# A recurrent branch's projection as seven block products, run two tiles at a time under attention

## The chip, the cores and the metric

One core of one Trainium2 chip runs the whole kernel. The metric is the device time of one execution in microseconds; for the kernel before it is 2162.91 us, the median of three runs (2162.57 to 2163.46).

The engines, by the names that the profile uses: PE is TensorE (matrix products; PEld is its loading of weights), DVE is VectorE, ACT is ScalarE, POOL is GpSimd, SP is SyncE, which only issues transfers. ACTq, POOLq and SPq are the queues from which ScalarE, GpSimd and SyncE issue transfers. Each engine has its own list of instructions, with semaphores between the lists. Sums of matrix products are formed in PSUM, in tiles of 128 x 512 numbers that this text calls banks.

## The reference

A decoder block over 2048 positions and 1024 channels, in float32. One input projection gives eight parts: the input and gate of a recurrent branch, queries, keys, values and a gate of an attention branch, and two merge gates.

```python
x_rnn, z_rnn, q, k, v, z_attn, g_r, g_a = jnp.split(h @ w_in, IN_SPLITS, axis=-1)
hr = rg_lru(causal_depthwise_conv(x_rnn, conv_w, conv_b), ...)
y_rnn = (hr * silu(z_rnn)) @ w_out_rnn            # 2048 x 1024 @ 1024 x 1024
o = dilated_attention_mixture(rope(q), rope(k), v)
y_attn = (o * silu(z_attn)) @ w_out_attn
merged = sigmoid(g_r + bg_r) * y_rnn + sigmoid(g_a + bg_a) * y_attn
x = x + gate * (merged @ w_o)
return rms_norm(x, g_final)
```

The change concerns `y_rnn`, the product with `w_out_rnn`.

## The kernel before

**Precision.** A number is split into a high and a low part, both of type float32r (`hi_act`, `hi_dve` or a VectorE reduction for the high part; `lo_pool` on GpSimd or `lo_dve` on VectorE for the rest), and a product of two such pairs is three matmuls, `mm3`: high x high, high x low, low x high. One `mm3` over 128 x 128 weights and 512 columns is called a step here.

**Positions** are held in four banks of 512 columns, n = 0 to 3. The input projection is done in two halves f = 0, 1 of two banks each. `values_half` forms the values (and, in `build_odd`, the operands of the odd bank and the sums `T1` to `T4`); then 28 pairs of weight columns follow in `strassen`, seven block products each where plain blocks would need eight. Their weight operands are split on the way (tiles `S`, a ring of `NS` = 7). In the second half the operands of the first 20 pairs come back from a copy in DRAM, `sD`, loaded by `load_next` as ring tiles come free. `recurrent` finishes the recurrent branch and stores it, transposed, in DRAM as `yaT` (1024 x 2048).

The order of the work is written out: `late` and `after_prod` list functions to be called after the nth block product (`n_prod`), `later(d, fn)` puts one d products ahead. `values_half` is the exception: there a scheduler orders the instructions.

In the second half more is put beside the products. `output_weights` loads both output projections' weights, splits them and stores the pairs to DRAM in `wD` (one half tile every four products: load at 1, split at 4, store at 5, with the split held in the one-buffered tiles `s1`, `s2`). `residual_gate` forms the residual gate's row from `w_mod`.

**Attention** comes next, in slots: a list of 96 units (16 heads and halves, six units each) runs through stages several slots apart. In each slot TensorE does the scores of one unit, the transposes of a unit seven slots older and the weighted sums of one eight slots older; VectorE and ScalarE do the softmax and copy out of PSUM. Between them the generator `fill` is advanced: it is the output projection, one step at each `next`. `FILL` says how many steps a slot is owed; `spend` takes them at three places of a slot, two after the scores and one after the transposes.

`fill` is made by `steps(jobs)`. A job is a bank n of one branch; a tile is 128 rows m of its output, eight steps over k, summed in one of two PSUM banks of the pool `pjb` (tiles `pj`). The weights come by `load_w` (one transfer of 512 KB for four steps, three tiles ahead, four buffers), the operand by `load_y` and `split_y` (256 KB per k, once for each bank). `evict` multiplies a finished sum by its gate (`load_g`) with VectorE, at step 1 of the next tile, and `store` writes it to `mrT`. The jobs are the four banks of `yaT`, then four of `oT` (the attention branch). The first five banks, 320 steps, go under attention and a few steps of them behind it; the last three run afterwards with other work, and then comes the final projection with w_o.

```python
fill = steps([(0, yaT, n) for n in range(NB)] + [(1, oT, n) for n in range(NB)])
...
mm3(ps[:], wt[:, 0, k % KH, :], wt[:, 1, k % KH, :], yh[:], yl[:], first=k == 0, last=k == KT - 1)
```

## Time and profile before

| | us |
|---|---|
| median of three runs | 2162.91 |
| the profiled execution | 2161.23 |
| its span, first to last instruction | 2159.4 |
| PE busy | 2136.6 (99%) |
| PEld busy | 1788.3 (83%) |
| DVE busy | 1463.3 (68%) |
| ACT busy | 1296.2 (60%) |
| POOL busy | 1120.6 (52%) |

The mean granted TensorE clock is 0.998. The stages lie so: the first half's values and products to about 690 us, the second half's values to 785, its products to 1340, attention with the projection beside it from 1340 to 1866, the rest of the projection to 1999, the final projection to the end.

How to read rows: a group is "line engine operation, output<-inputs by the program's names, partitions x elements, xcount | busy us, mean ns of one | idle time of the engine just before them, and what ended it". A row of busy times by stage is "from:to length, busy us (xinstructions) of PE, PEld, DVE, ACT and POOL, granted clock, share of the DMA engines' time, GB/s". A row of waits is "who <- whom: us in total, times, longest". A timeline row is "start, us, engine, line, operation, tiles, xcount [idle before]". L152 is `mm`, L163 `hi_dve`, L166 `lo_pool`, L169 `lo_dve`, L160 `hi_act`, L1795 `evict`, L1777 the high part in `split_y`, L1480 the softmax's first pass.

### The profile page before, as it was taken

The numbers are of one execution on the slowest core, as the hardware profiler recorded it, in microseconds if no ns is written. First come the engines' busy times: TensorE is split into PE (matmuls) and PEld (weight loads), VectorE is DVE, ScalarE is ACT, GpSimd is POOL, SyncE is SP. The second block draws the span as 40 slices with busy tenths as digits, with TensorE's granted clock in tenths as the row PEclk, the third lists the DMA queues.
The fourth block names the chain that finished last, engine by engine and source line by source line (L and its number), as shares of the span: only waits on it lengthen the run. The fifth ranks groups of instructions, "written<-read, shape, count | busy, mean of one in ns | idle before, by whom it ended". The sixth has DMA issues, their size and how long they took to land.

```text
span 2159.4 us, 32571 instructions
## 1 busy us (share of the span) xinstructions
PE 2136.6 (99%) x10539; PEld 1788.3 (83%) x10539; DVE 1463.3 (68%) x2582; ACT 1296.2 (60%) x2592; POOL 1120.6 (52%) x868
## 2 busy tenths in 40 slices
PE   9999999999999999999999999999999999999998
PEld 6888778888888888888888887889898988878887
DVE  6759878768656715544436684587777687788777
ACT  5748668668644527457457532677788888443333
POOL 1467667777666423223223675466666664432555
PEclk9999999999999999999999999999999999999999
DMA  8467887887655368899997676888887777899543
GB/s 301 142 211 256 280 290 264 288 294 244 174 115 166 108 229 291 301 305 311 323 318 240 152 173 171 300 269 263 273 275 218 256 236 239 300 316 300 181 170 114
DMA packets 416575, 521.39 MB, mean 241 GB/s; under 512 B 107574, under 2 KB 282898, under 8 KB 415380
## 3 DMA queue, kind: packets, MB, share of 16 engines
q1 hardware_dynamic: 376388, 401.65, 59.7%
q10 hardware_dynamic: 34384, 99.78, 12.2%
q0 software_dynamic: 5632, 17.88, 2.6%
q8 instruction: 83, 1.36, 0.3%
q14 instruction: 88, 0.72, 0.1%
HBM read 332.02 MB, written 187.17 MB: 240 GB/s over the span
## 4 chain that ended last, share of the span: by engine, by line
PE 71%; DVE 4%; DMA 3%; issue 1%; POOL 1%; ACT 1%; SPq 0%; ACTq 0%; POOLq 0%; DVEq 0%
PE X L152 14%; PE V L152 13%; PE pj L152 12%; PE Z L152 7%; PE W L152 7%; PE Y L152 6%; PE sc L152 4%; PE o L152 4%; PE pg L152 1%; PE pT L1568 1%; PE pT L1581 1%; DMA fg<-gaT 1%; DMA kraw<-kqT 1%; DVE ptl L169 1%; DVE yl L169 1%
## 5 line engine op out<-in xcount | busy, mean ns | idle before, releaser
L166 POOL TENSOR_TENSOR S<-R,S 128x512 fp32r<-128x512 f32 x192 | 295.3, 1546 | 169.3 <-ACT S L160 82.9
L152 PE MATMUL V<-T,S 128*128 128x512 f32 x1344 | 324.3, 390 | 1.9 <-DVE ev L461 1.9
L152 PE MATMUL X<-T,S 128*128 128x512 f32 x1344 | 323.8, 390 | 1.6 <-ACT u L391 1.3
L152 PE MATMUL pj<-yh,S 128*128 128x512 f32 x896 | 321.6, 402 | 1.3 <-DVE fg L1795 0.8
L152 PEld LDWEIGHTS X<-T,S 128*128 128x128 f32 x1344 | 251.8, 188 | 56.5 <-ACT u L391 2.9
L152 PEld LDWEIGHTS V<-T,S 128*128 128x128 f32 x1344 | 251.9, 188 | 55.9 <-issue 1.9
L166 POOL TENSOR_TENSOR S<-s,S 128x512 fp32r<-128x512 f32 x116 | 173.3, 1494 | 150.1 <-ACT S L160 114.3
L152 PEld LDWEIGHTS pj<-yh,S 128*128 128x128 f32 x896 | 168.3, 188 | 32.3 <-DVE S L169 1.3
L1481 ACT ACTIVATE pp<-pp,st 128x256 f32<-128x256 f32 (+3 forms) x256 | 133.8, 524 | 78.0 <-DVE st L1480 77.4
L152 PE MATMUL pj<-yl,S 128*128 128x512 f32 x448 | 175.5, 392 | 1.0 <-POOL yl L166 1.0
L160 ACT ACTIVATE S<-s 128x512 fp32r<-128x512 f32 x124 | 77.3, 624 | 145.1 <-DVE s L291 92.1
L152 PE MATMUL W<-T,S 128*128 128x512 f32 x672 | 161.6, 389 | 0.0
L152 PE MATMUL Y<-T,S 128*128 128x512 f32 x672 | 161.6, 389 | 0.0
L152 PE MATMUL Z<-T,S 128*128 128x512 f32 x672 | 161.4, 389 | 0.0
L160 ACT ACTIVATE S<-R 128x512 fp32r<-128x512 f32 x200 | 121.5, 622 | 59.0 <-DMA R<-in_w_in_dram 14.8
L169 DVE TENSOR_TENSOR ptl<-pT,pth 128x384 fp32r<-128x384 f32 (+1 forms) x160 | 97.8, 628 | 80.5 <-ACT pth L160 78.4
L152 PEld LDWEIGHTS W<-T,S 128*128 128x128 f32 x672 | 126.0, 188 | 26.9 <-issue 0.9
L152 PEld LDWEIGHTS Z<-T,S 128*128 128x128 f32 x672 | 126.2, 188 | 26.2
L152 PEld LDWEIGHTS Y<-T,S 128*128 128x128 f32 x672 | 126.1, 188 | 26.1
L166 POOL TENSOR_TENSOR s<-R,s 128x512 fp32r<-128x512 f32 x32 | 43.2, 1350 | 188.8 <-ACT s L160 164.6
L980 DVE SCALAR_TENSOR_TENSOR xc<-xr,par,xc 128x512 f32<-128x512 f32 x96 | 102.0, 1062 | 52.1 <-ACT xc L974 49.9
L1548 ACT ACTIVATE pp<-pp,M 128x256 f32<-128x256 f32 (+3 forms) x256 | 118.0, 523 | 12.8 <-DVE M L1680 12.8
(419 smaller groups left out, 4906.0 us busy)
## 6 DMA issues: line engine op xcount, KB each, us to landing
sD<-S ACTq DMA_DIRECT2D x140, 512.0 KB, 3.7
S<-sD SPq DMA_DIRECT2D x140, 512.0 KB, 5.0
S<-wD SPq DMA_DIRECT2D x82, 512.0 KB, 5.5
R<-in_w_in_dram SPq DMA_DIRECT2D x144, 256.0 KB, 3.3
wD<-s ACTq DMA_DIRECT2D x64, 256.0 KB, 5.1
kraw<-kqT SPq DMA_DIRECT2D x32, 384.0 KB, 5.1
T<-in_w_mod_dram SPq DMA_DIRECT2D x16, 512.0 KB, 9.1
vN<-ev SPq DMA_DIRECT2D x32, 256.0 KB, 2.7
```

Source lines behind the costliest of these rows:

```text
L152: nc.tensor.matmul(o, lhsT=l, rhs=r, start=st, stop=sp, **kw)
L160: nc.scalar.activation(o, i, AF.Copy)
L166: nc.gpsimd.tensor_tensor(o, i, h.bitcast(F32), ALU.subtract)
L169: return nc.vector.tensor_tensor(o, i, h.bitcast(F32), ALU.subtract).ins
L980: nc.vector.scalar_tensor_tensor(xc, xr[:, i : i + CH], cw(i), xc, ALU.mult, ALU.add)
L1481: nc.scalar.activation(pdst, pdst, AF.Exp, bias=m_, scale=-1.0, accum_out=l_)
L1548: nc.scalar.activation(pp, pp, AF.Copy, scale=w)
L1568: nc.tensor.transpose(pt[:, c0 + j * P : c0 + (j + 1) * P], pp[i][:, k * P : (k + 1) * P], ident)
L1581: nc.tensor.transpose(pt[:, c * P : (c + 1) * P], pp[:, half * P : (half + 1) * P], ident)
```

## The change

The four banks of `yaT` become two pairs q = 0, 1. For each pair and each pair of weight row blocks the 2 x 2 blocks of output are formed from seven products of weight sums and operand sums instead of eight of plain blocks. One product has four steps for each of four row blocks p, so a group g (one of seven products of a pair) has 16 steps, and there are 14 groups.

- The weight sums are formed and split in `output_weights`, beside the second half's products, and stored in `wB`, 28 tiles; the attention weights stay as they were. A split comes every three products (`PITCH`) instead of four.
- The operand differences T1 to T4 of a pair are formed from `yaT` and stored in DRAM as `tB`: for the first pair on GpSimd among the values of the second half (`block_sums_early`, loads and stores on SyncE's queue), for the second on VectorE and GpSimd in groups of ten products at the end of the second half (`block_sums`, stores on ScalarE's queue).
- `residual_gate` works in two half rows, to make room.
- In `steps`, the 14 groups replace four of the jobs. Row blocks are interleaved, so that two sums are open at a time in the same two PSUM banks: steps 0, 1, 2, 5 belong to row block 0; 3, 4, 6, 7 to 1; 8, 9, 10, 12 to 2; 11, 13, 14, 15 to 3. A sum is evicted one step after its last. Operands are loaded (`operand`) and split (`split`) four a group, into seven pairs of tiles; from the eighth on the low parts are made on GpSimd.
- `FILL` goes from 2.85 and 2.75 steps a slot to 2.54 and 2.44.

```diff
-FILL = (2.85, 2.75)
+FILL = (2.54, 2.44)
...
+    wB = scratch("wB", [7, KH, P, 2, KH, P])
+    tB = scratch("tB", [2, 4, KH, P, CH])
...
+    BLOCKS = (("B11", 0), ("B21", 4), ("T2", 1), ("T3", 2), ("T1", 3), ("T4", 5), ("B22", 6))
+    N_WB = 2 * 7 * KH
+    def load_wb(x):
+        load_w_tile(wB[BLOCKS[x // KH % 7][1], x % KH])
...
     def output_weights():
+        n0, PITCH = n_prod[0], 3
...
+        def split_and_store(n, raw, dst):
...
+        for p in range(KH):
+            v, b = {}, 7 * PITCH * p + (4 * PITCH if p > 1 else 0)
+            load = block_loads([w_out_rnn[0][:, 2 * p * P : 2 * (p + 1) * P]])
+            for d, name, i, half in ((1, "a22", 1, 1), (4, "a21", 1, 0), (6, "a11", 0, 0), (8, "a12", 0, 1)):
...
+            for x, (i, name, *sums) in enumerate((
+                (5, "a22"), (3, "a22", "a21", "a22", ALU.add), (0, "a11"), (1, "a22", "a22", "a11", ALU.subtract),
+                (2, "a21", "a11", "a21", ALU.subtract), (4, "a12"), (6, "a12", "a12", "a22", ALU.subtract))):
+                if sums:
+                    on_n(b + 5 + PITCH * x, lambda combine=combine, name=name, sums=sums: combine(name, *sums))
+                split_and_store(b + 5 + PITCH * x, lambda v=v, name=name: v[name], wB[i, p])
...
     def values_half(f, xs):
...
-        for ws in wide_values(vx, 1, n0, (0, 1), None if f else ws1):
+        for x, ws in enumerate(wide_values(vx, 1, n0, (0, 1), None if f else ws1)):
             next(odd)
+            if f and x % 2:
+                block_sums_early(vx, x // 2)
         for x, _ in enumerate(wide_values(vx, 1, n1, (1, 0), ws)):
             for _ in range((1, 2, 1, 0)[x]):
                 next(odd)
+            if f and x % 2:
+                block_sums_early(vx, 2 + x // 2)
...
+    def block_sums_early(pool, k):
+        load, combine, store = block_sum_ops(pool, 3, 0, k)
+        load(*B11)
+        load(*B12)
+        combine(B11, B12, B11, nc.gpsimd)
+        store_t1 = lambda: store(0, B11, nc.sync)
+        load(*B22)
+        combine(B12, B22, B12, nc.gpsimd)
+        store(2, B12, nc.sync)
+        combine(B22, B22, B11, nc.gpsimd)
+        store_t1()
+        load(*B21)
+        combine(B21, B21, B22, nc.gpsimd)
+        store(1, B22, nc.sync)
+        store(3, B21, nc.sync)
...
+    def block_sums(pool):
+        dve, gps = nc.vector, nc.gpsimd
+        for k in range(KH):
+            load, combine, store = block_sum_ops(pool, 4, 1, k)
+            for d, fn, *args in ((-3, load, *B12), (-3, load, *B11), (-3, load, *B22), (-2, load, *B21),
+                                 (0, combine, B11, B12, B11, dve), (0, combine, B12, B22, B12, gps),
+                                 (1, combine, B22, B22, B11, dve), (2, store, 0, B11, nc.scalar), (2, store, 2, B12, nc.scalar),
+                                 (2, combine, B21, B21, B22, gps), (3, store, 1, B22, nc.scalar), (4, store, 3, B21, nc.scalar)):
+                later(4 + 10 * k + d, lambda fn=fn, args=args: fn(*args))
...
     def steps(jobs):
...
+        def split(n, raw=None):
+            if n < 14 * KH:
+                h, l = OT[n]
+                src = l[:].bitcast(F32) if raw is None else raw[:]
+                if raw is not None or n % 2 == 0 and n < 7 * KH:
+                    hi_act(h[:], src)
+                else:
+                    nc.vector.tensor_reduce(h[:], src.unsqueeze(2), AX.X, ALU.max)
+                (lo_dve if raw is not None and n > 4 else lo_pool)(l[:], src, h[:])
...
+        OUT = {"B21": (0, 0), "T1": (1, 1), "T4": (1, 0), "B22": (0, 1)}
...
+        def block_evict(g, p, ps):
+            name = BLOCKS[g % 7][0]
+            tt = nc.vector.tensor_tensor
+            if name == "B11":
+                U[p] = T(fl, [P, CH], F32, f"F{14 + p}")
+                nc.vector.tensor_copy(U[p][:], ps[:])
+            elif name in ("T2", "T1"):
+                tt(U[p][:], ps[:], U[p][:], ALU.add)
+            elif name == "T3":
+                Q[p] = T(pR, [P, CH], F32, f"R{p}")
+                tt(Q[p][:], ps[:], U[p][:], ALU.add)
+            if name in OUT:
+                t = G[g, p]
+                tt(ps[:], ps[:], (Q if OUT[name][0] else U)[p][:], ALU.add)
+                tt(t[:], ps[:], t[:], ALU.mult)
...
+        order = [divmod(x, 10) for x in (0, 1, 2, 10, 11, 3, 12, 13, 20, 21, 22, 30, 23, 31, 32, 33)]
+        for g in range(14):
+            for j, (p, k) in enumerate(order):
...
+                if j % KH == 1:
+                    y = KH * g + j // KH
+                    (load_wb(y + 3) if y + 3 < N_WB else load_w(y + 3 - N_WB))
...
+                w, (yh, yl) = W[x], OT[KH * g + k]
+                mm3(ps[p][:], w[:, 0, k, :], w[:, 1, k, :], yh[:], yl[:], first=k == 0, last=k == KH - 1)
+                if k == KH - 1:
+                    W.pop(x)
+                    for d, fn in ((1, block_evict), (3, block_store)):
+                        waiting.setdefault(divmod(16 * g + j + d, 16), []).append((fn, g, p, ps[p]))
+                for at_, k1 in ((1, 0), (4, 1), (7, 2), (11, 3)):
+                    if j == at_ and n + k1 > 6:
+                        operand(n + k1)
+                for at_, k1 in ((6, 0), (9, 1), (12, 2), (15, 3)):
+                    if j == at_ and n + k1 > 6:
+                        split(n + k1)
...
-    fill = steps([(0, yaT, n) for n in range(NB)] + [(1, oT, n) for n in range(NB)])
+    fill = steps([(1, oT, n) for n in range(NB)])
```

More of the change, by code (lines that the diff above doesn't have):

```diff
@@ new lines, in decoder_block, with block_sum_ops, load, combine @@
+    B11, B12, B21, B22 = (0, 0), (0, 1), (1, 0), (1, 1)
+    def block_sum_ops(pool, bufs, q, k):
+        raws = {}
+        def load(half, j):
+            n = 2 * q + j
+            raws[half, j] = t = T(pool, [P, CH], F32, "bs", bufs=bufs)
+            nc.sync.dma_start(t[:], yaT[(half * KH + k) * P : (half * KH + k + 1) * P, n * CH : (n + 1) * CH])
+        def combine(dst, a, b, eng):
+            eng.tensor_tensor(raws[dst][:], raws[a][:], raws[b][:], ALU.subtract)
+        def store(i, src, queue):
+            queue.dma_start(tB[q, i, k], raws.pop(src)[:])
+        return load, combine, store
@@ L1365, in decoder_block @@
             residual_gate(qp)
+            block_sums(qp)
         else:
@@ L1809, in steps, with run_block @@
+        rest = [f for n in sorted(waiting) for f in waiting[n]]
+        def run_block(i):
+            fn, *args = rest[i]
+            fn(*args)
         last = None
```

192 lines of the change are left out of this document (126 added, 66 removed).

## The prediction

> **What bounds the kernel now.** I read the page's engine totals first, then the timeline of a stretch of block products, then busy times by stage, then the costs of the operations that the change touches.
>
> ```profile
> span 2159.4 us, 32571 instructions
> ...
> PE 2136.6 (99%) x10539; PEld 1788.3 (83%) x10539; DVE 1463.3 (68%) x2582; ACT 1296.2 (60%) x2592; POOL 1120.6 (52%) x868
> ...
> L152 PE MATMUL X<-T,S 128*128 128x512 f32 x1344 | 323.8, 390 | 1.6 <-ACT u L391 1.3
> ```
>
> TensorE is busy 99% of the span. A busy matmul row is not yet a full pipeline, so the second view is the timeline of two products of twelve matmuls each, and with it one stretch of the late projection that holds almost nothing but `pj` matmuls:
>
> ```profile
> 1103.98 2.88 PE L152 MATMUL V<-T,S 128*128 128x512 f32 x12
> 1106.70 2.88 PE L152 MATMUL Z<-T,S 128*128 128x512 f32 x12
> ...
> 1925.00:1975.00 50.00, 50.00 (x222) 41.40 (x221) 44.34 (x72) 21.94 (x40) 15.75 (x30) 1.00 0.93 325
> ```
>
> Twelve matmuls take 1106.70 - 1103.98 = 2.72 us, 0.227 us each, though a single one is listed with 0.39. The projection runs at the same pace, 50 us / 222 = 0.225. There TensorE has no hole, so a matmul taken out is worth 0.227 us. The Trainium skill, "Perfetto Trace Analysis", Identifying the Most-Contended Engine, says the same of matmul rows: they overlap, and busy time misjudges them. By listed durations the saving below would read 96 x 0.39 = 37 us; by the pace it is 21.8, and this trace agrees with the page.
>
> The third view is busy time by stage (PE, PEld, DVE, ACT, POOL, then clock, DMA share and GB/s): all of the attention stage, quiet stretches, and four in which operands of the next bank are split.
>
> ```profile
> 1340.00:1866.00 526.00, 520.34 (x3363) 465.35 (x3362) 380.95 (x1099) 400.67 (x1114) 312.39 (x271) 1.00 0.82 259
> 1430.00:1490.00 60.00, 60.00 (x405) 54.16 (x404) 41.44 (x152) 46.73 (x154) 35.33 (x39) 1.00 0.83 261
> 1640.00:1740.00 100.00, 100.00 (x666) 91.16 (x665) 70.08 (x201) 86.22 (x215) 62.28 (x49) 1.00 0.76 239
> ...
> 1400.00:1425.00 25.00, 24.16 (x163) 21.41 (x163) 23.48 (x68) 18.48 (x60) 17.68 (x17) 1.00 0.92 287
> 1500.00:1525.00 25.00, 24.33 (x160) 21.22 (x159) 23.40 (x63) 16.05 (x53) 19.34 (x18) 1.00 0.88 264
> 1610.00:1640.00 30.00, 27.55 (x169) 24.46 (x168) 25.05 (x61) 22.48 (x56) 20.76 (x16) 0.94 0.76 238
> 1740.00:1770.00 30.00, 29.72 (x196) 26.39 (x194) 27.89 (x69) 22.96 (x57) 20.88 (x15) 1.00 0.81 268
> ```
>
> In quiet stretches VectorE is 70% busy and TensorE has no idle time. Where VectorE rises to 93-94% TensorE loses 0.84, 0.67 and 0.28 us; the 2.45 us of the third includes a clock of 0.94. So TensorE bounds attention too, and a VectorE near full costs it some 0.6 us in 25 to 30. I use that price below.
>
> **TensorE work removed.** The projection was 4 banks x 8 x 8 = 256 steps of three matmuls; it becomes 2 bank pairs x 7 products x 16 = 224. That is 32 x 3 = 96 matmuls fewer, 96 x 0.227 = **-21.8 us**. All `pj` matmuls in question lie in the attention stage, whose order is fixed (FILL falls from 2.85 to 2.54 steps a slot, so the steps still end in about the same slot).
>
> **Work added under attention.** Costs of its operations, and who waited:
>
> ```profile
> L1795 DVE TENSOR_TENSOR fg<-pj,fg 128x512 f32<-128x512 f32 x39 | 26.6, 683 | 0.0
> L1777 DVE TENSOR_REDUCE yh<-R 128x512 fp32r<-128x512 f32 x32 | 21.5, 677 | 0.0
> L169 DVE TENSOR_TENSOR yl<-R,yh 128x512 fp32r<-128x512 f32 x18 | 17.3, 967 | 0.6
> L166 POOL TENSOR_TENSOR yl<-R,yh 128x512 fp32r<-128x512 f32 x21 | 27.6, 1314 | 19.1 <-DMA vraw<-vN 5.6 <-DVE yh L1777 4.4 <-PE sc L152 3.2
> L160 ACT ACTIVATE yh<-R 128x512 fp32r<-128x512 f32 x5 | 3.1, 628 | 3.7 <-PE pj L152 3.6
> ...
> DVE ptl L169 <- ACT pth L160: 78.4, 45, 2.9
> DVE pth L163 <- PE pT L1581: 17.8, 23, 1.2
> DVE pp L1480 <- PE sc L152: 14.2, 10, 3.0
> PE pj L152 <- DVE fg L1795: 0.8, 1, 0.8
> ```
>
> Evictions: a tile needed one multiply, 32 in all. Now the seven products of one row block need 1 (B11), 2 (B21), 1 (T2), 1 (T3), 3 (T1), 2 (T4) and 2 (B22), 12 in all, times 4 row blocks and 2 pairs = 96. The 64 more cost 64 x 0.683 = 43.7 us of VectorE. Splits: 56 operands instead of 32. High parts on VectorE rise from 24 to 39 (+15 x 0.677 = 10.2), on ScalarE from 8 to 17 (+9 x 0.628 = 5.7). Low parts move to GpSimd: VectorE 15 to 2 (-13 x 0.967 = -12.6), GpSimd 17 to 54 (+37 x 1.314 = 48.6). Sums: VectorE +41, ScalarE +6, GpSimd +49. All of it lies beside TensorE, not on its path, as long as the queues keep up: over the stage VectorE goes from 381/526 = 72% to 422/504 = 84%, ScalarE from 76 to 81%, GpSimd from 59 to 72%. But the recurrent steps end after some 85 of about 107 slots (526/107 = 4.9 us each). In a quiet slot VectorE works 69% of 4.9 = 3.4 us, 0.24 of it evictions of the old kind, so 3.15 are attention's. A group of 16 steps lasts 16/2.54 = 6.3 slots, about 29.5 us, with 19.8 us of attention. To that come 2 or 4 high parts (1.4 or 2.7) and 12 evictions in a T1 group (8.2: 29 to 31 us, full), 8 in one of B21, T4 and B22 (5.5: 27 to 28, 93%), 4 in the rest (2.7: 24 to 25, 84%). So the eight first are like the bursts above and the six others halfway: 8 x 0.6 + 6 x 0.3 = **+6.5**, my value. Ends: 0, as nothing excludes that the steadier load stalls less than a burst, and 14 x 0.84 = 12, the worst burst at full clock in each group.
>
> **The two tiles in two banks.** Before, an evicted bank was needed eight steps later. Now row block 0 ends at step 5 of a group, its eviction is queued at step 6, and row block 2 takes the same bank at step 8. What stands in VectorE's queue then:
>
> ```profile
> 1701.12 0.42 DVE L1480 CUSTOM_DVE_ANT_0 pp<-sc,msk 128x256 f32<-128x256 f32 x1 [0.72 <-PE sc L152]
> 1702.53 0.08 DVE L1480 DVE_READ_ACCUMULATOR2_ANT st<- 128x1 f32 x1
> ...
> 1707.79 1.03 PE L1581 MATMUL pT<-cs,pp 128*128 128x128 f32 x8
> 1708.59 0.47 PE L152 MATMUL pj<-yh,S 128*128 128x512 f32 x1
> ```
>
> A slot has three spots for steps: two after the scores, one after the transposes. The worst case is step 6 first in a slot: the softmax (1702.61 - 1701.12 = 1.5 us) goes ahead of the eviction, and TensorE arrives at step 8 after two steps (1.36) and eight transposes (0.80), 2.16 us. A T1 eviction then is 1.5 + 2.05 - 2.16 = 1.4 us late, one with two operations 0.7, a single one not. Counting the owed steps slot by slot from FILL puts step 6 there in four of 14 groups (B11, T3, T1, T4). The other cases have sums and scores between, 2.6 us more. That makes 2 us, and transposes queued ahead of an eviction add some. Ends: 0, and 14 x 1.4 = 20 if each group is caught. I take **+3**.
>
> **Loads.** Per 16 steps SyncE issues about 12.6 transfers instead of 10, 4.24 instead of 3.58 MB; by steps per us and with attention's own transfers in 5% less time the stage's 259 GB/s becomes about 280, its share 0.82 about 0.89. Two loads a group (at steps 5 and 11) wait for the matmul of the same step, and gate and query loads queue behind them on SyncE for under a slot. Weights still come three tiles ahead. I take 0.
>
> **The differences among the values.** 16 GpSimd subtractions, 16 loads and 16 stores enter the value products of the second half, on SyncE's queue between weight loads and value stores.
>
> ```profile
> 700.00:787.00 87.00, 86.96 (x397) 71.19 (x396) 44.89 (x70) 40.91 (x75) 29.08 (x20) 1.00 0.43 132
> 744.15 0.69 DVE L619 TENSOR_TENSOR hx<-hx,T 128x512 f32<-128x512 f32 x1
> 744.76 1.79 DVE L169 TENSOR_TENSOR T<-t,T 128x512 fp32r<-128x512 f32 x1
> 744.19 3.50 POOL L166 TENSOR_TENSOR S<-R,S 128x512 fp32r<-128x512 f32 x2 [14.17 <-PE W L152]
> 734.70 0.68 DVE L169 TENSOR_TENSOR b12l<-hx,b12h 128x512 fp32r<-128x512 f32 x1
> 749.24 0.64 PE L152 MATMUL V<-S,b12h 128*128 128x512 f32 x2
> 765.05 0.69 DVE L169 TENSOR_TENSOR T<-t,T 128x512 fp32r<-128x512 f32 x1
> 785.18 2.88 PE L152 MATMUL Z<-T,S 128*128 128x512 f32 x12
> ```
>
> GpSimd goes from 29 to about 50 of 87 us, DMA from 132 to 132 + 8.4 MB/87 us = 228 GB/s. Beside a GpSimd subtraction a VectorE one takes 1.79 instead of 0.69 us. Sixteen such hits would make `build_odd` up to 17.6 us late; the last low part of B12 is done 14.5 us before its first matmul, the T operands 20 us before the second product. So it mostly fits; SyncE waiting for a subtraction with a weight load behind it is the other price, 0 to 4. I take **+1**.
>
> **In the second half's products.** Twelve more splits of output weights (28 + 16 for 32) every three products instead of four, 16 VectorE sums, more stores on ScalarE's queue; then ten-product groups of differences (8 subtractions each on VectorE and GpSimd) and the residual gate in half-rows.
>
> ```profile
> 1050.00:1150.00 100.00, 100.00 (x442) 82.73 (x441) 42.74 (x54) 51.34 (x81) 28.45 (x21) 1.00 0.97 321
> S<-sD SPq DMA_DIRECT2D x140, 512.0 KB, 5.0
> wD<-s ACTq DMA_DIRECT2D x64, 256.0 KB, 5.1
> 1140.00:1340.00 200.00, 200.00 (x878) 163.59 (x877) 130.65 (x155) 96.69 (x156) 115.41 (x78) 1.00 0.65 177
> ```
>
> TensorE has no hole here, and the engines have room. The transfers have the least: 0.97 share, with a third more output-weight traffic, about 30 GB/s. But operands are fetched seven tiles ahead, 16 us against 5.0 to land. The store of a split now has two products, 5.4 us, before its tile is rewritten, against 5.1 to land: ScalarE will wait at times, with copies out of PSUM and sigmoids queued behind it that have several products of time. Ends 0 and 7 (30 GB/s over 98 us at 400); I take **+0.5**.
>
> **Sum.** -21.8 + 6.5 + 3 + 1 + 0.5 = -10.8 us. The profiled execution took 2161.2 us (span 2159.4), 1.7 below the median of the runs, 2162.9. So 2161.2 - 10.8 = 2150.4, and as a median **2152**.
>
> **Rivals.** *All of it hides* (VectorE has 504 - 422 us left, and short bursts cost little): only the 21.8 stands, 2162.9 - 21.8 = 2141. 17%.
>
> *The shared port.* The VectorE row of 1.79 us beside a GpSimd row is a wait, not slower work. If all 16 early differences hit and SyncE adds its 4, B12 is 3.1 us late: 3 + 4 in place of 1, 2158. Against it: GpSimd has long idle pieces there. 12%. The Trainium skill, "SBUF", Who interferes with whom, has it as a lock: a VectorE operation with two SBUF inputs and a GpSimd one that reads SBUF exclude each other for a whole instruction. The 1.79 agrees; by that rule the new evictions, one input from PSUM, stay free of it.
>
> *Two banks are too few*: if every group is caught once by 1.3 us, 18 in place of 3, that gives 2162.9 - 21.8 + 6.5 + 18 + 1.5 = 2167, and with 12 in place of 3, two groups in three, 2161, no change that can be told. I give the milder form its chance. For it: only two banks and a VectorE near full; against it: one wait of 0.8 us in all before. 12%.
>
> *VectorE becomes the bound*, slower. Its in-order waits for ScalarE and TensorE, 78.4 + 17.8 + 14.2 = 110 us, stay as long as they are while 422 us of work pass: 532 against 526 us now, 6 us slower, 2169. It decides once over 104 of the 110 persist. Against it: in the bursts only 6-7% of idle time was left. 6%.
>
> The forecast has 53%, with 2146 to 2157 as its own range. Measurement tells 0.2% (4.3 us) from no change. Faster: 53 + 17 + 12 = 82%; no change 12%; slower 6%. The range reaches from the first rival to just short of no change: 2141 to 2160.
>
> **What would show it.** `pj` matmuls fewer by 96 in all; VectorE near 84% in attention, TensorE's `pj` waiting on evictions (a few us), attention about 10 us shorter, values and products unmoved within 2 us. The prediction is wrong if `pj`, `pT` or `o` matmuls wait over 15 us there, if a hole opens between 700 and 790 us, or if operand loads land later than 16 us after issue around 1100.

## The result, and the profile after

The changed kernel takes 2199.41 us (median of four runs, 2198.05 to 2200.42) against 2162.74 us for the kernel before in the same series: a ratio of 1.017, 95% interval 1.015 to 1.019. It is slower by 37 us where I predicted 11 us faster. The profiled execution took 2200.42 us:

```profile
PE 2137.8 (97%) x10443; PEld 1779.5 (81%) x10443; DVE 1554.7 (71%) x2680; ACT 1306.0 (59%) x2613; POOL 1221.0 (56%) x941
```

TensorE has 96 matmuls fewer (10539 before) and the same busy time, so some of them ran longer. I cut both traces at the same events: the first value matmul of the second half, the first block product behind the values, the first `pj` matmul, the last `o` matmul. All lengths below are between these marks.

| stage, us | before | after | difference | predicted |
|---|---|---|---|---|
| values, second half | 99.2 | 113.4 | +14.2 | +1 |
| products, second half | 557.9 | 569.1 | +11.2 | +0.5 |
| attention | 522.3 | 534.0 | +11.7 | -12.3 |
| everything else | 980.0 | 982.1 | +2.1 | 0 |
| span | 2159.4 | 2198.6 | +39.2 | -10.8 |

Of the 50 us between the forecast and this trace attention holds 24.0, the values 13.2, the products 10.7 and the rest 2.1.

Busy times by stage, first of the kernel after, then of the kernel before (PE, PEld, DVE, ACT, POOL, granted clock, DMA share, GB/s):

```profile
684.00:797.00 113.00, 102.32 (x456) 82.94 (x455) 63.70 (x80) 49.22 (x87) 61.95 (x44) 0.94 0.64 203
735.00:760.00 25.00, 14.62 (x50) 11.00 (x49) 24.86 (x27) 10.95 (x19) 13.13 (x9) 0.73 0.58 183
1306.00:1366.00 60.00, 58.32 (x254) 46.92 (x253) 46.41 (x51) 12.88 (x23) 40.40 (x25) 1.00 0.72 209
1366.00:1426.00 60.00, 49.24 (x232) 40.63 (x231) 31.12 (x93) 27.47 (x82) 23.68 (x22) 0.89 0.83 272
1366.00:1900.00 534.00, 507.41 (x3245) 449.25 (x3244) 414.27 (x1160) 404.24 (x1122) 353.28 (x305) 0.98 0.80 260
```

```profile
683.00:782.00 99.00, 98.96 (x457) 81.09 (x456) 51.74 (x80) 48.44 (x87) 38.60 (x28) 1.00 0.47 147
1280.00:1340.00 60.00, 60.00 (x260) 47.75 (x260) 34.16 (x45) 16.22 (x29) 35.44 (x24) 1.00 0.63 173
1340.00:1400.00 60.00, 58.74 (x331) 50.34 (x330) 31.16 (x106) 33.36 (x107) 21.95 (x22) 1.00 0.89 291
```

The number of matmuls in the values is the same, but between 735 and 760 TensorE has a hole, and the clock falls to 0.73. At the products' end VectorE went from 34 to 46 of 60 us. In attention's first 60 us TensorE does 232 matmuls instead of 331, at a clock of 0.89. So the loss lies in three places, and in each the granted clock falls with it. The record of the clock has seven stretches at half speed outside the program's end, 41 us in all, against one of 3.4 us before. Matmuls ran in 32 us of them, which lost 16.1 us, against 1.7 before: **14 of the 39 us are half clock**.

**The values.** ScalarE's timeline, then VectorE's and TensorE's, of the kernel after; last, one row of ScalarE before:

```profile
734.10 0.64 ACT L162 ACTIVATE T<-hx 128x512 fp32r<-128x512 f32 x1 [4.33 <-DVE hx L654]
...
739.20 0.63 ACT L162 ACTIVATE T<-hx 128x512 fp32r<-128x512 f32 x1 [3.94 <-DVE hx L657]
...
745.46 0.63 ACT L162 ACTIVATE T<-t 128x512 fp32r<-128x512 f32 x1 [1.92 <-DVE t L661]
...
747.92 0.58 ACT L898 ACTIVATE ev<-X 128x512 f32<-128x512 f32 x1
...
737.39 1.77 DVE L657 TENSOR_TENSOR hx<-hx,hx 128x512 f32<-128x512 f32 x1
...
748.55 2.08 PE L154 MATMUL X<-S,T 128*128 128x512 f32 x4 [8.15 <-ACT ev L898]
```

```profile
737.28 0.58 ACT L863 ACTIVATE ev<-X 128x512 f32<-128x512 f32 x1
```

A finished value sum `X` waits in PSUM; its copy `ev` stands in ScalarE's queue behind splits of the odd bank's operands, and these wait for VectorE, which takes 1.77 us for what took 0.69. The copy comes at 747.92 instead of 737.28, and the next matmul on that bank waits 8.15 us. Between 700 and 765 VectorE has 21 operations over 1.3 us instead of 9; together its operations take 22.0 us over their 0.69 instead of 9.9. So VectorE spends 12 us more on the same operations.

**The products.** VectorE, then TensorE:

```profile
1281.51 1.77 DVE L1187 TENSOR_TENSOR t<-t,St 128x512 f32<-128x512 f32 x1
1283.20 1.77 DVE L1314 SCALAR_TENSOR_TENSOR gacc<-gw,ca,gacc 128x512 f32<-128x512 f32 x1
1284.90 1.77 DVE L1345 TENSOR_TENSOR bs<-bs,bs 128x512 f32<-128x512 f32 x1
1286.59 1.75 DVE L1190 TENSOR_TENSOR t<-t,t 128x512 f32<-128x512 f32 x1
1288.27 1.75 DVE L306 TENSOR_TENSOR s<-R,s 128x512 f32<-128x512 f32 x1
1289.94 0.68 DVE L496 TENSOR_TENSOR t<-V,u 128x512 f32<-128x512 f32 x1
...
1290.76 5.46 PE L154 MATMUL V<-T,S 128*128 128x512 f32 x12 [3.81 <-DVE t L496]
```

The copy of a product out of its bank (L496) stands behind five operations of 1.75 to 1.77 us in a row. Two of them are a half-row addition of the residual gate (L1314) and a late subtraction (L1345), the others work that the kernel before has too; GpSimd works beside them from 1279.74 to 1289.47 without a break. TensorE waits 3.81 us, and its next twelve matmuls take 5.46 us instead of 2.88.

**Attention.** VectorE and TensorE at the start, then the waits of TensorE over the whole stage:

```profile
1380.47 1.29 DVE L171 TENSOR_TENSOR kq<-kraw,kq 128x512 fp32r<-128x512 f32 x2 [4.91 <-ACT kq L162]
1381.68 0.68 DVE L1941 COPY F<-pj 128x512 f32<-128x512 f32 x1
...
1382.41 1.65 PE L154 MATMUL pj<-F,S 128*128 128x512 f32 x3 [3.83 <-DVE F L1941]
...
1408.49 0.69 DVE L1918 TENSOR_REDUCE F<-F 128x512 fp32r<-128x512 f32 x1 [5.72 <-DMA F<-tB]
...
1410.57 1.65 PE L154 MATMUL pj<-F,S 128*128 128x512 f32 x3 [4.34 <-DVE fg L1950]
```

```profile
PE pj L154 <- DVE fg L1950: 7.2, 4, 4.3
PE pj L154 <- DVE F L1941: 4.1, 2, 3.8
PE sc L154 <- POOL q L1530: 4.0, 3, 3.0
```

Two evictions stand behind something that waits for a transfer: the first head's keys, and an operand `F` whose load came late. To measure the many small waits too, I took the starts of successive matmuls less the pace of each shape (0.227 us for 512 columns); what is over is called stall below, time lost to half clock included. Attention's stalls went from 35.6 to 70.5 us, 3.1 to 18.5 of them in the first 60 us; the pace of its matmuls alone gives 23.1 us less than before (843 `pj` matmuls lie in the stage instead of 945; six of the 102 moved behind it).

### The profile page after: what moved, and what is told of

The parts are those of the page before. It is cut to its first block, busy times and chain, and to the rows that moved or that the text cites. A ratio compares the mean times of both kernels' runs of the same rounds, so it can differ in the third digit from the quotient of the medians.

```text
span 2198.6 us, 32865 instructions
## 1 busy us (share of the span) xinstructions
PE 2137.8 (97%) x10443; PEld 1779.5 (81%) x10443; DVE 1554.7 (71%) x2680; ACT 1306.0 (59%) x2613; POOL 1221.0 (56%) x941
## 5 line engine op out<-in xcount | busy, mean ns | idle before, releaser
L154 PE MATMUL pj<-F,S 128*128 128x512 f32 x1248 | 335.3, 405 | 16.5 <-DVE fg L1950 7.2
L154 PEld LDWEIGHTS pj<-F,S 128*128 128x128 f32 x1248 | 226.7, 192 | 61.8 <-DVE fg L1950 9.4
L168 POOL TENSOR_TENSOR s<-R,s 128x512 fp32r<-128x512 f32 x44 | 59.7, 1356 | 204.0 <-ACT s L162 61.5
L162 ACT ACTIVATE S<-R 128x512 fp32r<-128x512 f32 x200 | 121.9, 622 | 65.2 <-DMA R<-in_w_in_dram 14.5
L1568 DVE CUSTOM_DVE_ANT_0 pp<-sc,msk 128x256 f32<-128x256 f32 (+3 forms) x256 | 103.0, 447 | 8.3 <-PE sc L154 7.7
```

The costliest lines, as they stand in the source:

```text
L154: nc.tensor.matmul(o, lhsT=l, rhs=r, start=st, stop=sp, **kw)
L162: nc.scalar.activation(o, i, AF.Copy)
L168: nc.gpsimd.tensor_tensor(o, i, h.bitcast(F32), ALU.subtract)
L1568: nc.vector.tensor_tensor_reduce(pdst, s_ps, mask, 1.0, 3e38, ALU.add, ALU.min, m_)
```

## Experiments

Edits in different stages went into one kernel and are read by stage; k stands for the changed kernel's own lengths in the first row. "Start" and "rest" are attention's stalls in its first 60 us and after. e2, e4, f2, g2 and i1 leave work out of the computation; the others do all of it. Each row is read from the trace of one execution.

| run | values | products | attention | start | rest |
|---|---|---|---|---|---|
| k, the change | 113.4 | 569.1 | 534.0 | 18.5 | 52.0 |
| before | 99.2 | 557.9 | 522.3 | 3.1 | 32.5 |
| e1_split_roles | 108.2 | 579.8 | 537.2 | 13.9 | 59.8 |
| e2_less_work | 109.9 | 563.0 | 521.4 | 16.4 | 41.4 |
| e4_no_early_sub | 104.6 | 567.2 | 537.3 | 16.9 | 56.8 |
| f1_late_diffs_banks | 114.6 | 570.0 | 532.9 | 17.0 | 52.4 |
| f2_static_subs | 108.7 | 564.1 | 524.2 | 13.8 | 46.9 |
| f3_more_evict (of before) | 99.2 | 557.9 | 537.3 | 5.7 | 45.0 |
| g1_mended | 99.6 | 598.9 | 529.5 | 17.6 | 48.3 |
| g2_light | 113.7 | 558.7 | 515.7 | 12.6 | 39.5 |
| h1_front_keys | 108.9 | 571.1 | 533.4 | 17.4 | 52.5 |
| h2_front_all | 108.5 | 570.3 | 528.4 | 15.0 | 49.9 |
| i1_lightest | 104.0 | 559.0 | 518.4 | 12.8 | 42.1 |
| j1_thin_slots (of before) | 99.1 | 558.0 | 526.2 | 5.8 | 36.4 |
| j2_thick_first | 113.0 | 573.1 | 535.7 | 17.4 | 54.8 |
| j3_more_at_start | 110.5 | 572.9 | 539.8 | 16.0 | 59.6 |

**What a hole costs.**

```diff
+            for n, m in ((22, 1), (52, 3), (82, 5), (112, 13)):
+                after_prod.setdefault(n_prod[0] + n, []).append(lambda m=m: hole(rp, m))
```

> The kernel before with four holes for TensorE in the second half's products, 30 products apart: a matmul waits for a chain of 1, 3, 5 and 13 VectorE operations on a bank, about 1, 2.5, 4 and 9.5 us. If a hole costs its length alone, the time rises by the holes' sum, about 17 us, and the granted clock stays at 1.0. If TensorE's clock falls behind a hole, stretches of 3.4 or 6.8 us at half clock follow the longer ones, and the time rises by 5 to 9 us more. Where the shortest hole brings none, the point from which it starts lies between.

2194.20 us against 2161.30, 32.9 more. TensorE's rows at the four holes:

```profile
849.07 0.22 PE L152 MATMUL pg<-hole 128*32 128x32 f32 x2 [1.77 <-DVE hole L1299]
849.22 4.47 PE L152 MATMUL Z<-T,S 128*128 128x512 f32 x12
...
943.10 0.29 PE L152 MATMUL pg<-hole 128*32 128x32 f32 x2 [3.24 <-DVE hole L1299]
...
1037.20 0.28 PE L152 MATMUL pg<-hole 128*32 128x32 f32 x2 [4.71 <-DVE hole L1299]
...
1136.23 0.28 PE L152 MATMUL pg<-hole 128*32 128x32 f32 x2 [10.57 <-DVE hole L1299]
```

Even the 1.77 us hole is followed by 3.4 us at half clock, and its twelve matmuls take 4.47 us. At the others the stretches are 6.8, 6.8 and 10.2 us, all three begun inside the hole. The waits sum to 21.5 us (with one of 1.25 ahead of the second hole), and 9.3 us went to half clock in the four stretches. So the clock's part of the changed kernel's loss is a consequence of its holes, not a thing of its own. The Trainium skill, "TensorE: Matmul & The Clock Gate", Part 1: The HAM clock gate, gives the half rate after at least one idle window of some 3.4 us; here one of 1.77 us was enough, while one of 1.78 us at 297.5 us of the same run brought none.

**Values: transfers or subtractions.** Two edits try to free SyncE's queue, one takes the subtractions out, one keeps them without their transfers.

```diff
# e1: loads and stores of the early differences on GpSimd's queue (and: late subtractions on VectorE; odd low parts on VectorE)
-        load, combine, store = block_sum_ops(pool, 3, 0, k)
+        load, combine, store = block_sum_ops(pool, 3, 0, k, nc.gpsimd)
# e2: value stores on ScalarE's queue (and: late subtractions left out; additions of the recombination left out)
+        (nc.scalar if n > 1 else nc.sync).dma_start(vN[...
-                tt(ps[:], ps[:], (Q if OUT[name][0] else U)[p][:], ALU.add)
# e4: early subtractions left out (and: late ones all on GpSimd; row blocks one after the other)
-        combine(B11, B12, B11, nc.gpsimd)
...
+        order = [... (0, 1, 2, 3, 10, 11, 12, 13, 20, 21, 22, 23, 30, 31, 32, 33)]
# f2: the same 16 subtractions on two still tiles (and: gate additions left out; hi_act for every operand)
+            nc.gpsimd.tensor_tensor(still[1][:], still[0][:], still[0][:], ALU.subtract)
```

> Three edits in three stages of the changed kernel, each read by the length of its own stage. Values of the second half (99.2 us before, 113.4 after): loads and stores of the early differences go through GpSimd's queue instead of SyncE's. If SyncE's order is the cause (difference loads that wait for buffers hold up the value stores behind them), 99 to 102 us. If the subtractions on GpSimd themselves slow VectorE down, 110 to 114. Products of the second half (557.9 before, 569.1 after): all 16 late subtractions on VectorE, none on GpSimd. If the wait of VectorE for GpSimd fills VectorE, 559 to 562; if it is the number of VectorE operations, 569 or more. Attention (522.3 before, 534.0 after): odd low parts on VectorE instead of GpSimd. If GpSimd is too full, 524 to 529; if VectorE's queue is what is late, 535 to 540.

> Three edits in three stages of the changed kernel. Values (113.4 us after): only the stores of the values go to ScalarE's queue, behind their own evictions; the differences stay on SyncE. If the value stores behind waiting difference loads are the cause, 99 to 102 us; if GpSimd's subtractions are, 110 to 114; in between if weight loads behind the same loads count too. Products (569.1 after): the late subtractions are left out, loads and stores stay. Both theories on VectorE say 558 to 562; if the weight splits every three products or the gate in half rows are the cause, 566 to 569. Attention (534.0 after): evictions cut to one operation each (the additions of the recombination left out, 40 VectorE operations or 27 us less). If VectorE's work is what costs, 515 to 522; if the operand loads and the start of the stage are, 528 to 533.

> Three edits in three stages of the changed kernel. Values (113.4 us after): the 16 early subtractions on GpSimd are left out, loads and stores stay on SyncE. If GpSimd's subtractions slow VectorE, 99 to 102 us; if SyncE's order is the cause, 104 to 113 (a difference's buffer is free sooner without its subtraction, so some of it goes in any case). Products (569.1 after): all 16 late subtractions on GpSimd. If VectorE's wait for GpSimd fills it, 570 to 575; if the number of VectorE operations does, 560 to 565. Attention (534.0 after): row blocks one after the other instead of interleaved (a bank is then used again three steps after its last matmul instead of two, the last operand is loaded a step later). If two banks are too few, 520 to 528; if not, 532 to 538.

> Three edits in three stages of the changed kernel. Values (113.4 us after): the 16 subtractions stay on GpSimd but work on two tiles that never change, without the loads and stores of differences (the differences themselves aren't formed; a plain copy takes their place in DRAM). If GpSimd's subtractions alone cost, 108 to 113; if the transfers do, 99 to 102. Products (569.1 after, 563.0 without the late subtractions): the additions of the residual gate are left out, all but the first of each half, so 14 VectorE operations fewer. If VectorE's fullness at the end of the stage is the cause, 557 to 562; else 566 or more. Attention (534.0 after, 521.4 with 40 VectorE operations fewer): all high parts on ScalarE instead of VectorE, 39 operations moved. If only VectorE is short, 520 to 526; if ScalarE is as short, 533 to 545.

I had read the hole as SyncE's order: value stores behind loads of differences that wait for buffers. That theory fell. With the value stores on ScalarE's queue (e2) the same hole is there:

```profile
749.35 0.58 ACT L898 ACTIVATE ev<-X 128x512 f32<-128x512 f32 x1
...
749.99 0.79 PE L154 MATMUL X<-S,T 128*128 128x512 f32 x1 [8.14 <-ACT ev L898]
```

Without the subtractions (e4) the values take 104.6 us and VectorE's lateness is as before (9.5 us, nine slow operations); with the subtractions but no transfers (f2) they take 108.7. So subtractions alone cost 9.5 us, transfers alone 5.4, together 14.9 against 14.2 for both; single executions tell this to some 2 us (below). The part of the transfers in e4, on ScalarE and SyncE:

```profile
749.01 0.60 ACT L898 ACTIVATE ev<-W 128x512 f32<-128x512 f32 x1 [2.73 <-DMA vN<-ev]
...
742.45 0.32 SPq L1342 DMA_DIRECT2D bs<-yaT  x1
746.12 0.32 SPq L1348 DMA_DIRECT2D tB<-bs  x1
746.48 4.29 SPq L899 DMA_DIRECT2D vN<-ev  x4
```

Here the value store does wait behind the differences, and a copy waits for its buffer. i1, below, shows that another queue does not mend it. e1 has 108.2 us, between what its two theories said, and gave a wait of 4.5 us to the first products in exchange (its 579.8 has some 8 us of that).

In the **products** I expected one of VectorE's wait for GpSimd and the number of VectorE's operations to win. All late subtractions on VectorE made 572 (579.8 less those 8), all on GpSimd 567.2; kernels with the same products as the change lie between 569.1 and 573.1, and h2, with all of them on GpSimd, at 570.3, so shifting them between the engines tells nothing. Leaving them out made 563.0, leaving out gate additions 564.1: 5 to 6 us each. In **attention** odd low parts on VectorE took 3.2 us more, and the row blocks one after the other 3.3, which is no more than the products differ between like kernels; fewer additions brought 12.6, high parts on ScalarE 9.8.

**Putting the early differences elsewhere, and more banks.**

```diff
# f1: differences called beside the last value products; four banks in the first two groups
+                    ps[p] = T(pT, [P, CH], F32, "pT") if g < 2 and p > 1 else T(pj, [P, CH], F32, "pj")
# g1: on VectorE, held back behind the odd bank's last operand (and e2's value stores, e4's late subtractions, f2's high parts)
+            with tc.issue_after(last_odd[0]):
+                for k in range(KH):
+                    block_sums_early(vx, k)
# h1: differences at the head of the stage; key low parts of the first head on GpSimd
-            (lo_pool if self.f or self.h or c == 2 else lo_dve)(KQ[...
+            lo_pool(KQ[...
```

> Two edits in two stages of the changed kernel, with the whole computation. Values (99.2 us before, 113.4 after, 104.6 without the early subtractions): the early differences are all put behind the last operand of the odd bank, beside the last value products, where VectorE has no operands left to build. If GpSimd's subtractions cost because they slow VectorE's building of operands, behind which ScalarE's value eviction stands, 99 to 103 us; if the transfers of the differences or SyncE's order cost, 108 or more. Attention (534.0 after; its first 60 us hold 18.5 us of TensorE stalls against 3.1 before): in the first two groups row blocks 2 and 3 are summed in the two banks of the transposes, idle then, so that no bank is used again within a group. If two banks are too few at the start, the first 60 us lose 8 us or more of their stalls and the stage ends 6 to 12 us sooner; if late operands and key loads hold it, 2 us or less.

> The whole computation of the changed kernel with four edits: the early subtractions on VectorE and held back until the last operand of the odd bank is built (values), the value stores on ScalarE's queue (values), all late subtractions on GpSimd (products), all high parts of operands on ScalarE (attention). If the two causes found for the values (VectorE slowed beside GpSimd, value stores behind difference loads) are the whole of it, the values take 99 to 103 us instead of 113.4, the products 566 to 568 instead of 569.1, attention 523 to 527 instead of 534.0, and the kernel 2172 to 2178 us, 1.004 to 1.008 of before. If the held-back subtractions only move the delay to the start of the products, 2180 to 2188.

> Two edits in two stages of the changed kernel, with the whole computation. Values (113.4 us after; 99.6 with the subtractions held back, which then held up the products by 21 us): the early differences are put at the head of the stage, ahead of the odd bank's operands. If only the overlap of the subtractions with the building of operands costs, 100 to 105 us and no hole at the start of the products; if the sixteen loads and stores cost wherever they stand, 107 or more. Attention (534.0 after, 18.5 us of stalls in its first 60 us): the low parts of the first head's keys on GpSimd instead of VectorE, so that nothing on VectorE ahead of the first evictions waits for the keys. If that place in VectorE's queue is what holds the first sums, the wait of 3.8 us for the first copies goes and the first 60 us lose 5 to 8 us; if late operands do, 0 to 2.

f1 says nothing on the values: the scheduler put the subtractions where they had been (the first at 702, the last at 763 us). Nor does g2 (below), which held them back on GpSimd: they ran from 701 to 762 us, and the values took 113.7 us where 99 to 104 had been expected. In g1 they did move, and the values took 99.6 us, as before; but there is a hole of 21 us among the first products. 13 of the 16 loads went between 775 and 829, VectorE's subtractions wait for them (8.4 us for one), and the copies of the first products out of their banks stand behind these subtractions: the matmul after the hole waited 21.25 us for such a copy. Busy times of g1, values and then the first products:

```profile
687.00:786.00 99.00, 98.89 (x455) 80.72 (x454) 56.81 (x85) 48.77 (x87) 38.34 (x28) 1.00 0.53 165
786.00:832.00 46.00, 21.68 (x87) 17.12 (x85) 8.91 (x13) 1.79 (x3) 0.00 (x0) 0.74 0.74 245
```

g1 took 2212.23 us, 1.023 of before (1.020 to 1.025): the delay was moved and grew. h1 gained 4.5 us, but its subtractions began 16 us into the stage, as in the change, so it does not tell its theories apart either. (j2 and j3, with the values of the change, took 113.0 and 110.5 us, f1 and g2 114.6 and 113.7: 4 us between like kernels, so a difference of that size says little here.)

On the start of attention: counting waits over 0.15 us, four banks cut those of `pj` matmuls in the first 60 us from 15.8 to 4.4 us (and 1.8 on the borrowed banks). Yet all stalls fell only from 18.5 to 17.0, for the waits at the scores rose from 0.8 to 9.6; by what f1 had set out, two banks are not what holds the start. h1 shows the same: the wait for the first copies went, and this came:

```profile
PE sc L154 <- ACT kq L162: 5.2, 1, 5.2
```

The first head's keys are late. Their last stores are issued 4.2 us after the first `pj` matmul instead of 1.5, where VectorE is fuller, and the loads land 13 to 15 us after it instead of 9 to 13. Whatever needs them first, sum or score, waits.

**The added VectorE work by itself, and thinner slots by themselves,** both in the kernel before:

```diff
# f3
+            for _ in range(2 if t < 32 else 0):
+                nc.vector.tensor_scalar(ps[:], ps[:], 1.0, None, ALU.mult)
# j1
-FILL = (2.85, 2.75)
+FILL = (2.54, 3.05)
```

> The kernel before with two more VectorE operations on the bank ahead of each eviction of the recurrent branch, 64 of 0.68 us or 44 us in all, which is what the change's evictions add; nothing else is altered, and a bank is needed only eight steps later. By the price that I predicted with, the attention stage (522.3 us) grows by 3 to 7 us. If VectorE's fullness costs more than that, by 10 to 25; if the steady part of the change's loss is owed to the two banks instead, by 0 to 3.

> The kernel before with fewer projection steps in attention's first 55 slots (2.54 a slot instead of 2.85, as in the change) and more in the later ones (3.05 instead of 2.75), no work added or removed. If the steps taken away also took away cover (VectorE and ScalarE have less TensorE time in a slot to finish a softmax), TensorE's stalls in the attention stage rise by 4 to 10 us from 35.6, most of them in its first three fifths, and the kernel is 3 to 8 us slower. If only the added work counts, stalls stay within 2 us and so does the time.

f3's attention stage by busy times:

```profile
1344.00:1881.00 537.00, 522.38 (x3346) 461.68 (x3344) 418.16 (x1160) 397.47 (x1109) 308.72 (x268) 1.00 0.79 252
```

44 us more on VectorE make the stage 15.0 us longer, with VectorE at 78% and banks that aren't needed for eight steps. That is about the change's 414 us on VectorE. Behind the first 60 us f3 has 12.5 us more stalls than the kernel before, the change 19.5, so this is the larger part of its steady loss. j1 adds nothing and has 6.6 us more stalls (35.6 to 42.2): the steps taken out of a slot had covered the softmax. Its time, 2168.58 us beside 2166.21, is one pair of runs and says little; the stalls say it, and j2, below, moves them the other way.

**Does it add up?**

```diff
# g2: e2's and f2's edits on products and attention together
# i1: g2, without early subtractions, value stores on ScalarE's queue, key low parts on GpSimd
```

> Work left out of the changed kernel, to see whether the costs add up: in the products both the late subtractions and all but the first addition of each half of the residual gate, in attention the additions of the recombination, with all high parts on ScalarE too; the early subtractions stay on GpSimd, held back behind the odd bank's last operand. If VectorE's fullness is the only cause, the products take 557 to 559 us (569.1 less 6.1 less 5.0; before 557.9) and attention 510 to 514 (534.0 less 12.6 less 9.8). If another engine or the loads set the rest, products 562 or more and attention 517 to 521. Values 99 to 104 if only the overlap with the building of operands matters.

> All suspected costs of the change left out or moved at once, to see whether anything else is hidden: values without the early subtractions (the differences are not formed) and with the value stores on ScalarE's queue; products without the late subtractions and all but the first addition of each half of the gate; attention without the additions of the recombination, high parts on ScalarE, and the first head's key low parts on GpSimd. If GpSimd's subtractions and the value stores behind difference loads are the whole of the values' loss, 99 to 101 us; if something else is there, 103 or more. Products 557 to 560 (558.7 measured). Attention 515.7 without the edit on the keys: 508 to 512 if the place of the keys' low parts in VectorE's queue holds the first sums when the keys come in time, 514 to 518 if the late keys themselves do. The kernel 2156 to 2163 us, against 2161 before.

The products do: 558.7 and 559.0 us without subtractions and gate additions, 557.9 before. Attention with both edits is 515.7, some 4 us above the sum of the single gains; part of f2's 9.8 was probably the lighter end of the products (g1 and h2, with full products and high parts on ScalarE, took 529.5 and 528.4). The values stayed at 104.0, and so the queue was not what made the transfers cost; that is 3 us over the 101 that a full explanation would have given. ScalarE in i1, and where the value stores stand among the transfers of i1 and of before (last column: median us to landing):

```profile
745.46 0.60 ACT L898 ACTIVATE ev<-W 128x512 f32<-128x512 f32 x1 [3.54 <-DMA vN<-ev]
```

```profile
vN<-ev ACTq DMA_DIRECT2D x15, 256.0 KB, 5.3
```

```profile
vN<-ev SPq DMA_DIRECT2D x14, 256.0 KB, 2.7
```

With 32 more transfers a store lands after 5.3 us instead of 2.7 (4.4 in e4, on SyncE's queue as before), and with two buffers the copies wait for that. Moving the keys' low parts changed nothing at the start (12.6 and 12.8 us). i1 took 2166.51 us beside 2162.85: even with the suspected work left out the change does not win, for 12.8 + 42.1 = 54.9 us of stalls remain against 35.6.

**More steps at the start, and everything that helped.**

```diff
# j2
-FILL = (2.54, 2.44)
+FILL = (2.85, 2.05)
# j3 (with f2's high parts)
-FILL = (2.54, 2.44)
+FILL = (2.54, 2.30)
-MORE = 0.8
-FIRST = 4.0
+MORE = 1.6
+FIRST = 6.0
# h2: h1, with the value stores on ScalarE's queue, late subtractions on GpSimd, high parts on ScalarE, four banks
```

> The changed kernel with the old 2.85 steps a slot in the first 55 slots and 2.05 instead of 2.44 in the later ones. If thin slots are part of the loss, the first three fifths of attention stall less and the rest more: 534.0 us changes by less than 4, but the stalls move. At the start (18.5 us of stalls in 60), a few steps more before the first scores take 2 to 5 us off if late keys are what is waited for, and nothing if evictions and operands are.

> The changed kernel with all high parts on ScalarE (attention 524.2, 13.8 us of stalls in the first 60) and two more steps in slot 0 and 0.8 more in each of slots 0 to 6, taken from the slots after 55. If the start stalls because scores and keys come late with too few steps to cover them, the first 60 us lose 3 to 7 us and attention takes 518 to 522; if the steps themselves wait (operands, evictions), the first 60 us stall as much or more and attention takes 524 to 530.

> The whole computation with all edits that helped a stage: early differences at the head of the values, value stores on ScalarE's queue, late subtractions on GpSimd, key low parts on GpSimd, high parts of operands on ScalarE, four banks for the first two groups. If the gains add up: values 100 to 104, products 566 to 568, attention 516 to 522 (9.8 less for the high parts, 5 to 8 for the keys), the kernel 2165 to 2175 us. It beats the kernel before (2161 to 2163) only if attention falls below 510. If GpSimd, which takes more, becomes what is late, attention stays at 524 to 532.

More steps at the start took 1 us off its stalls in j2. j3 has 16.0 there, beside 13.8 in f2, which comes to the start from lighter products, and 17.6 in g1, which does not; its whole stage took 539.8 us, longer than either theory said. So more steps did not cure the start. In j2 the stalls behind the first 300 us of the stage rose from 21.1 to 27.8, those between 60 and 300 us fell from 30.9 to 27.0, as thin slots would have it. h2 took 2191.66 us beside 2160.53, where single gains added up had given 2165 to 2175; it is still the best version with the whole computation. No version here beats the kernel before.

## Why the prediction was wrong, point by point

- **TensorE work removed, -21.8: right as far as it goes.** 96 matmuls are gone, and by the pace of its matmuls attention is 23.1 us lighter, 1.4 of it moved behind the stage. But I gave the removed steps no other role; j1 shows that they were cover, 6.6 us of it.
- **Work added under attention, +6.5 (its own terms give 6.6): mis-sized.** f3 measures 15.0 for the evictions alone. I had taken 0.6 us per burst of VectorE at 93 to 94% and set aside the largest row, 2.45 us, because it included a clock of 0.94. That clock was part of the price. VectorE's work came out as forecast (414 us, forecast 422).
- **Two tiles in two banks, +3:** the waits were there (behind the first 60 us `pj` matmuls stall 8.0 us against 1.4), but neither more banks at the start nor the other order made the stage shorter by over 1.1 us. More banks behind the start were not tried, so a few us there stay open.
- **The start of attention: not in the sum.** 15.4 us more stalls in 60 us, with half clock in it. f3 and j1 give 2.6 and 2.7 of them; the rest goes with the late keys and with late operands such as the `F` above, issued at 1400.18 and used at 1408.49. Which part belongs to which is open.
- **The differences among the values, +1: the step that failed most clearly.** That subtractions hold VectorE up was right, and so was the size (up to 17.6 us said, 12 measured). The cover was wrong: I asked when the odd bank's operands are needed, 14.5 us later (13.9 from the end of the row that I read), and not what else stands behind the same steps in ScalarE's queue. The value copies did, with no cover. The transfers beside them (5.4 us) I had priced only as a wait of SyncE.
- **In the second half's products, +0.5: wrong.** "The engines have room" was a mean over 200 us; in the last 60 VectorE had 34 us of work and got 46, with GpSimd beside it. The end I gave it, 7, was for transfers, which weren't the cause: g2 keeps the loads and stores of the late differences, and its products take 558.7 us. How much of the loss is the number of operations and how much their slowing beside GpSimd stays open.
- **Loads, 0:** at the weights right; at the operands wrong in the first 60 us.
- **The clock: missing altogether.** 14 of 39 us; e3 shows that holes bring it, one of 1.77 us already, though not every hole so short.

The rival nearest to it, a VectorE that becomes the bound (2169), had its sign and its engine, but not its places. The shared port had the mechanism of the values, with a price of 3 us for the subtractions, which alone cost 9.5, and 4 for SyncE's order, which another queue did not mend. Two of the signs that I had named for a failure came: a hole between 700 and 790, and `pj` and transpose matmuls that wait over 15 us in attention, 20.1 us by the view of waits.

## What to carry to other kernels

When a step makes an engine late, list everything that stands behind it in the queues of the engines that wait for it, and give each its own cover; the consumer that one thinks of is often not the first to starve. Price a hole of TensorE at its length and half of the slow stretch that follows, where one does. Matmuls taken out from beside other work take cover away too, so what they save is less than their time, and work given to an engine that is at 72% is not free: here it cost a third of its length.

## What was not expected of the hardware

- TensorE's clock halves after holes far shorter than I would have thought: 1.77 us idle brought 3.4 us at half clock, 3.24 and 4.71 us brought 6.8. In the seventeen traces of this case, between the program's start and its end, each of the 51 holes over 2.7 us had a slow stretch begin in it or within 5 us behind it, and 37 of the 60 of 1.7 to 2.7 us that did not lie in such a stretch. All changes of the clock there lie, within one trace, a multiple of 3.41 us apart; whether the place of a short hole between two of these moments decides was not tested.
- VectorE operations with two inputs in SBUF go from 0.69 to 1.77 us beside a GpSimd subtraction, as the prediction said; twelve more operations over 1.3 us went with 12 us more of its time. The Trainium skill, "SBUF — State Buffer", Who interferes with whom, has this exclusion; f2, whose subtractions have no transfers and still leave VectorE 20.3 us over instead of 9.9, agrees with it.
